# Prompt tokens in three groups (256, 384, 384) instead of four (128, 128, 384, 384), with split operands and the sample tokens in the first

## The chip, the core and the metric

The kernel runs on one core of a Trainium2 chip. The metric is the device time of one execution in microseconds (us); lower is better. Three runs of the kernel before took 4751.45, 4752.73 and 4761.79 us, with a median of 4752.73 us.

## What is computed

One step of a hybrid decoder layer for 1024 prompt tokens and 8 sample tokens of width 1024, in float32. A combined projection feeds three mixers (a state space scan with a convolution of 4 taps, a gated convolution of 31 taps, attention to 256 memory rows); their gated sum is projected and normalised. Then each token picks 128 of 16384 experts and adds what they return. Cut to what matters here:

```python
def _peer_block(t, w_q, sub_keys, u_tab, v_tab):
    qv = (t @ w_q).reshape(nt, PEER_HEADS, 2, PEER_DHALF)
    s = jnp.einsum('thkd,hknd->thkn', qv, sub_keys)
    s_top, i_top = lax.top_k(s, PEER_TOPK)
    ...
    best, pos = lax.top_k(cand.reshape(nt, PEER_HEADS, PEER_TOPK * PEER_TOPK), PEER_TOPK)
    gate = jax.nn.softmax(best.astype(jnp.float32), axis=-1).astype(t.dtype)
    u = jnp.take(u_tab, idx, axis=0)
    act = jax.nn.gelu(jnp.einsum('td,thkd->thk', t, u), approximate=False)
    v = jnp.take(v_tab, idx, axis=0)
    return jnp.einsum('thk,thkd->td', gate * act, v)

def _hybrid_layer(x, ...):
    proj = x @ w_in
    z, xbc, dt_raw, conf_in, q_mem, gates = jnp.split(proj, [...], axis=-1)
    ...
    merged = g[:, :, 0] * branch_a + g[:, :, 1] * branch_b + g[:, :, 2] * branch_c
    x = _layer_norm(ALPHA * x + merged @ w_out, ln1_g, ln1_b)
    x = _layer_norm(ALPHA * x + _peer_ffn(x, ...), ln2_g, ln2_b)
```

The state space scan and both convolutions carry a state from token to token, so the prompt has to be worked through in order.

## The kernel before, in words

**Groups.** The prompt is cut into groups (`GROUPS`), each of which goes through the whole layer up to its experts. `front(g)` (line 442) loads the group's tokens and works out the step sizes; `main(G)` (line 510) runs the mixers and the output projection. Every group loads every weight block anew: 88 blocks of the combined projection (`proj`, line 428), 16 of `wso`, 8 each of `wmo`, `wco` and `wo` (`out_product`, line 487), and 16 of `wq` (`routing`, line 685). A block is 128 x 1024 float32, 512 KB, in one of four buffers (`wr`).

**Products.** `product` (line 189) has two forms. With plain float32 operands (line 197) a block is eight matmuls, each of which the trace shows as two records. With a pair of float32r parts (line 186) the scalar engine rounds the block to `wh` (line 175), the vector engine takes the rest as `wl` (line 177), and three matmuls per eighth, 24 a block, add up `wh xh + wh xl + wl xh`. Before, the projections of groups 0 and 1 (`PLAIN`) are plain, those of the groups of 384 are split; the output products are plain in every group.

**Experts.** For all groups but the last the experts are fetched row by row. A *row* is one of a token's 128 choices for 128 tokens at once: the POOL queue gathers 128 x 1024 float32 from the table (line 404), and the vector engine multiplies and sums it (line 413 for `u`, line 423 for `v`). The 640 tokens of the groups ahead of the last have 640 `u` rows and 640 `v` rows; the samples add 16 of each. Five buffers (`uv`) hold rows. The last group's experts are done densely: `dense_group` (line 1126) multiplies by the whole tables, 128 blocks of each.

**What sets the order.** The program is written as a stream, and a scheduler turns it into one fixed list per engine. Work that fills gaps hangs on queues: `tick` (line 212) emits the next steps of `bg` (the memory's keys and values, then the routing of the group before), `TICKS[g]` steps a chunk of the scan; `side` holds the sample tokens' mixers, `PTICK[g]` steps a projection, from the group after the one with which the samples ride (`RIDE`). `spread` (line 237), called at each product, emits as many expert rows as a rate says: `PHASES[g]` by the part of `main`, `PACE` afterwards. Rows of a group exist once its routing is through. What is left when the dense work has been written is emitted at the end:

```python
    dense_group(G)
    while experts:
        due[0] = 8.0
        spread()
    sample_final()
```

**The samples' convolution state.** `sample_mixers` loads and stores it in three pieces each (lines 886 and 895); a piece is 128 x 64 runs of three floats.

## Time and profile before

| | us |
|---|---|
| median of three runs | 4752.73 |
| span of the profiled execution | 4755.2 |
| lowest, highest run | 4751.45, 4761.79 |
| busy in the span: PE, DVE, ACT, POOL | 4060.0, 3651.7, 1809.1, 1800.8 |

The profiled execution is the span from its first to its last instruction; it lies between the runs' lowest and highest time, so nothing of note lies around it. PE is the tensor engine, PEld its weight loads, DVE the vector engine, ACT the scalar engine, POOL the engine whose queue issues the gathers, SP the one whose queue issues all other transfers. Matmuls overlap in the profile: the start of one to the start of the next says what one costs, not its duration.

### The profile page before, as it was taken

Reading aid. Unit: us, or ns where it says so; the run is one execution under the profiler, and the core shown is the slowest. Engines: PE = TensorE matmul, PEld = TensorE weight load, DVE = VectorE, ACT = ScalarE, POOL = GpSimd, SP = SyncE. Lnnn points to the kernel's source line nnn. Section 1 sums busy time; section 2 is a strip of 40 time slices with the busy share of each in tenths; the row PEclk is TensorE's granted clock in tenths of the full one; section 3 lists DMA queues with packets and bytes.
Section 4 is the critical chain, followed back from the end, with each engine's and each line's share of the span. In section 5 each row is a group of like instructions: output and inputs, shape, how many; then the busy total and the mean of one; then the engine's idle time right before and its main releaser. Section 6 shows DMA issues by size and latency. Waiting matters only on the chain. (4 is left out here: it accounts for less than half of the span.)

```text
span 4755.2 us, 61836 instructions
## 1 busy us (share of the span) xinstructions
PE 4060.0 (85%) x20483; PEld 3296.9 (69%) x20483; DVE 3651.7 (77%) x7682; ACT 1809.1 (38%) x4128; POOL 1800.8 (38%) x1595
## 2 busy tenths in 40 slices
PE   9999961589878899899769898889887899789997
PEld 8999860578666776577448686545555688677886
DVE  1363561668898799789988899879886799788998
ACT  3434420136456332154225432221786333323334
POOL 0000030443533334554134644554111455555663
PEclk9999885889978999989888799889898999999999
DMA  6676689887847877987566876987567999999998
GB/s 200 211 237 223 204 275 52 306 306 258 289 158 233 260 272 268 359 280 251 180 230 209 322 250 221 339 298 266 189 216 268 323 389 389 255 349 366 371 383 300
DMA packets 500161, 1278.29 MB, mean 269 GB/s; under 512 B 111312, under 2 KB 182864, under 8 KB 497664
## 3 DMA queue, kind: packets, MB, share of 16 engines
q0 software_dynamic: 186880, 679.56, 40.7%
q1 hardware_dynamic: 312960, 594.77, 39.3%
q8 instruction: 162, 2.65, 0.2%
q14 instruction: 159, 1.30, 0.1%
HBM read 1220.22 MB, written 53.93 MB: 268 GB/s over the span
## 5 line engine op out<-in xcount | busy, mean ns | idle before, releaser
L404 POOL DMA_INDIRECT uv<-in_peer_u,idx x640 | 789.8, 1234 | 1198.4 <-DVE uv L413 804.5
L404 POOL DMA_INDIRECT uv<-in_peer_v,idx x640 | 841.7, 1315 | 899.6 <-DVE pacc L423 547.8
L413 DVE SCALAR_TENSOR_TENSOR uv<-uv,x 128x1024 f32<-128x1024 f32 (+1 forms) x656 | 789.5, 1218 | 198.9 <-DMA uv<-in_peer_u,idx 186.0
L423 DVE SCALAR_TENSOR_TENSOR pacc<-uv,av,pacc 128x1024 f32<-128x1024 f32 (+1 forms) x650 | 831.9, 1280 | 98.6 <-DMA uv<-in_peer_v,idx 87.4
L186 PE MATMUL mm<-xt,wh 128*128 128x384 f32 x2816 | 790.5, 361 | 22.5 <-ACT b L589 12.7
L197 PE MATMUL mm<-b,wr 128*128 128x128 f32 (+2 forms) x3072 | 746.6, 397 | 32.0 <-ACT b L648 9.9
L197 PEld LDWEIGHTS mm<-b,wr 128*128 128x128 f32 x3072 | 491.8, 200 | 239.5 <-issue 26.1
L175 ACT ACTIVATE wh<-wr 128x1024 fp32r<-128x1024 f32 x274 | 290.2, 1060 | 830.7 <-DMA wr<-in_win 250.1
L186 PEld LDWEIGHTS mm<-xt,wh 128*128 128x128 f32 x2816 | 538.8, 200 | 58.4 <-ACT b L589 17.6
L186 PE MATMUL mm<-xt,wl 128*128 128x384 f32 x1408 | 502.0, 357 | 36.0 <-DVE wl L177 35.9
L197 PE MATMUL mm<-xt,wr 128*128 128x128 f32 (+1 forms) x2816 | 371.7, 292 | 98.2 <-DMA wr<-in_win 91.3
L535 DVE SCALAR_TENSOR_TENSOR b<-raw,cc,b 128x128 f32<-128x128 f32 (+1 forms) x960 | 443.1, 478 | 11.7 <-ACT b L533 4.7
L197 PEld LDWEIGHTS mm<-xt,wr 128*128 128x128 f32 x2816 | 357.7, 204 | 107.7 <-issue 92.3
L177 DVE TENSOR_TENSOR wl<-wr,wh 128x1024 fp32r<-128x1024 f32 x274 | 333.3, 1217 | 32.7 <-ACT wh L175 32.2
L186 PEld LDWEIGHTS mm<-xt,wl 128*128 128x128 f32 x1408 | 280.7, 199 | 47.8 <-DVE wl L177 42.0
L1223 PE MATMUL mm<-wh,b 128*128 128x512 f32 x768 | 246.0, 402 | 16.7 <-ACT b L150 16.4
L150 ACT ACTIVATE b<-acc 128x384 fp32r<-128x384 f32 x128 | 66.7, 525 | 372.7 <-PE st L1223 224.5
L186 PE MATMUL sp<-b,wh 128*128 128x384 f32 x784 | 206.2, 345 | 0.5 <-ACT b L682 0.5
L186 PE MATMUL tp<-b,wh 128*128 128x384 f32 x784 | 202.6, 340 | 0.0
L1162 PEld LDWEIGHTS mm<-e,e 128*128 128x128 f32 x768 | 119.9, 208 | 95.1 <-ACT e L1161 83.8
L1223 PE MATMUL ss<-wh,b 128*128 128x512 f32 x512 | 182.9, 398 | 0.0
L197 PE MATMUL mm<-acc,wr 128*128 128x128 f32 (+3 forms) x640 | 153.0, 402 | 27.0 <-DVE acc L591 12.7
(386 smaller groups left out, 6880.1 us busy)
## 6 DMA issues: line engine op xcount, KB each, us to landing
wr<-in_win SPq DMA_DIRECT2D x352, 512.0 KB, 4.6
wr<-in_peer_ut SPq DMA_DIRECT2D x128, 512.0 KB, 7.1
e<-in_peer_v SPq DMA_DIRECT2D x256, 256.0 KB, 7.2
wr<-in_wso SPq DMA_DIRECT2D x64, 512.0 KB, 4.8
wr<-in_wq SPq DMA_DIRECT2D x64, 512.0 KB, 5.5
gd<-xt SPq DMA_DIRECT2D x16, 1536.0 KB, 5.1
xt<-gd SPq DMA_DIRECT2D x16, 1536.0 KB, 18.9
wr<-in_wmo SPq DMA_DIRECT2D x32, 512.0 KB, 5.2
```

The costliest lines, as they stand in the source:

```text
L150: act.activation(hi, src, AF.Copy)
L175: act.activation(wh, wr, AF.Copy)
L177: dve.tensor_tensor(wl, wr, f32(wh), op=OP.subtract)
L186: pe.matmul(ps, a[:, k], b[k0 + k], start=(i == 0), stop=(i == n - 1))
L197: pe.matmul(ps, w[:, k], xs[k], start=(k == 0), stop=(k == 7))
L404: pool.indirect_dma_start(out=dst, out_offset=None, in_=table, in_offset=bass.IndirectOffsetOnAxis(ap=idx_col, axis=0))
L413: dve.scalar_tensor_tensor(u, u, 1.0, x1, op0=OP.mult, op1=OP.mult, accum_out=av[:, s:s + 1])
L423: dve.scalar_tensor_tensor(acc, v, av[:, s:s + 1], acc, op0=OP.mult, op1=OP.add)
L535: dve.scalar_tensor_tensor(cv, raw[:, i:i + nt], col(C_FW, j * TAPS + i), cv, op0=OP.mult, op1=OP.add)
L1162: pe.matmul(pg[:, u * P:(u + 1) * P], oj[:, u], oi[:, u], start=True, stop=True)
L1223: pe.matmul(outs[2 * tbk + dh], a[:, ts], v[:, dh * 512:dh * 512 + 512], start=(c == 0 and i == 0), stop=(c == P - 1 and i == 2))
```

## The change

The two groups of 128 become one of 256; the groups of 384 stay. No group is plain any more, so the first group's projections are split too. The samples (8 columns) ride with group 0, which makes its projections 264 columns wide; their mixers are emitted in the group after, as before. The rates lose their entry for the second group of 128; those of the groups of 384 and of the dense part are the same. The functions keep their code; line numbers fall by 2 or 3.

```diff
-GROUPS = (128, 128, 384, 384)
+GROUPS = (256, 384, 384)
-PLAIN = (0, 1)
-TICKS = (8, 5, 2, 3)
-PTICK = (0, 0, 1, 0)
+TICKS = (4, 2, 3)
+PTICK = (0, 1, 0)
 PHASES = tuple(dict(zip(("ssd", "out0", "out1", "att", "merge", "rest"), x)) for x in (
     (0, 0, 0, 0, 0, 0),
-    (3.5, 3, 3, 3, 3, 3),
     (2.5, 4.5, 3, 3.5, 3, 2),
     (3.5, 2, 3, 4.5, 1, 3)))
-RIDE = 1
+RIDE = 0
...
-        xt = [xtp.tile([P, 8, N], dt, name="xt") for dt in ((F32,) if g in PLAIN else (F32R, F32R))]
+        xt = [xtp.tile([P, 8, N], F32R, name="xt") for _ in range(2)]
         xt = [[x[:, k, :nx] for k in range(8)] for x in xt]
-        raw = xt[0] if g in PLAIN else [blk(nx) for _ in range(8)]
+        raw = [blk(nx) for _ in range(8)]
         for k in range(8):
             sp.dma_start(raw[k][:, :nt], I["xT"][k * P:(k + 1) * P, G.t0:G.t0 + nt])
             if g == RIDE:
                 act.activation(raw[k][:, nt:], xs_raw[:, k], AF.Copy)
-            if g not in PLAIN:
-                split(raw[k], nx, hl=(xt[0][k], xt[1][k]))
-        G.x = raw if g in PLAIN else tuple(xt)
+            split(raw[k], nx, hl=(xt[0][k], xt[1][k]))
+        G.x = tuple(xt)
```

What the scheduler makes of it at three places. The vector engine's list from the dense part's results (line 1230) to its end, before; `uv` are rows of experts, `wr` the dense results, `x_35560` the samples' result:

```order
L1230 SCALAR_TENSOR_TENSOR wr<-wr,mm 128x512 x3
L390 TENSOR_REDUCE ln2d<-wr 128x1
...
L401 SCALAR_TENSOR_TENSOR wr<-wr,ln2d,wl 128x1024
L398 SCALAR_TENSOR_TENSOR wr<-wr,ln2d,wl 128x1024
L398 SCALAR_TENSOR_TENSOR x_35560<-x_35560,ln2s,uv 8x1024
L401 SCALAR_TENSOR_TENSOR wr<-wr,ln2d,wl 128x1024
L401 SCALAR_TENSOR_TENSOR x_35560<-x_35560,ln2s,uv 8x1024
```

The same stretch of the change (its line 1227 was 1230, its 411 and 421 were 413 and 423):

```order
L1227 SCALAR_TENSOR_TENSOR wr<-wr,st 128x512
L399 SCALAR_TENSOR_TENSOR wr<-wr,ln2d,wl 128x1024
L411 SCALAR_TENSOR_TENSOR uv,av<-uv,x_30912 128x1024
...
L411 SCALAR_TENSOR_TENSOR uv,av<-uv,x_30912 128x1024 x55
L414 TENSOR_TENSOR av<-av,gate_16095 128x128
L419 TENSOR_SCALAR pacc<-uv,av 128x1024
L421 SCALAR_TENSOR_TENSOR pacc<-uv,av,pacc 128x1024
...
L421 SCALAR_TENSOR_TENSOR pacc<-uv,av,pacc 128x1024 x3
...
L421 SCALAR_TENSOR_TENSOR pacc<-uv,av,pacc 128x1024 x123
L1239 SCALAR_TENSOR_TENSOR uv<-uv,pacc 128x1024
```

Before, no row of experts stands behind the dense part's first result; now 62 `u` rows and 128 `v` rows do.

The SP queue around the samples' convolution state (`sconv`), before, at the end of group 1; `wr` are weight blocks:

```order
L169 DMA wr<-in_win 128x1024 x3
L886 DMA sb<-in_sconv 128x64x3
L895 DMA out_sconv<-sb 128x64x3
L169 DMA wr<-in_win 128x1024
L886 DMA sb<-in_sconv 128x64x3 x2
L169 DMA wr<-in_win 128x1024
L895 DMA out_sconv<-sb 128x64x3 x2
L169 DMA wr<-in_win 128x1024
L169 DMA wr<-in_wmo 128x1024
```

And in the change, near the end of group 0:

```order
L167 DMA wr<-in_wco 128x1024
L167 DMA wr<-in_win 128x1024
L883 DMA sb<-in_sconv 128x64x3
L892 DMA out_sconv<-sb 128x64x3
L883 DMA sb<-in_sconv 128x64x3 x2
L892 DMA out_sconv<-sb 128x64x3 x2
L167 DMA wr<-in_wco 128x1024
L167 DMA wr<-in_win 128x1024
```

The same six transfers still stand between weight blocks of the first 256 tokens, now with no block between them.

The vector engine's first rows of experts, before, in group 1, between the chunks of its scan (`acc`, `sp_v` to `sp_w`: output products and the samples' step sizes):

```order
L732 TENSOR_TENSOR sp_v<-sp,dtb 8x32
L413 SCALAR_TENSOR_TENSOR uv,av<-uv,x_5265 128x1024 x4
L577 TENSOR_TENSOR acc<-acc,mm 128x128
L735 TENSOR_SCALAR sp_u<-sp_e 8x32
L413 SCALAR_TENSOR_TENSOR uv,av<-uv,x_5265 128x1024
```

And in the change, in the first group of 384 (`s_xdt`, `s_y`: the samples' state; 128x384: the group's blocks):

```order
L842 TENSOR_TENSOR b<-b 128x384 x4
L175 TENSOR_TENSOR wl<-wr,wh 128x1024 x2
L411 SCALAR_TENSOR_TENSOR uv,av<-uv,x_9274 128x1024
L919 SCALAR_TENSOR_TENSOR sb<-sb,s_xdt 128x128 x2
L922 SCALAR_TENSOR_TENSOR sb,s_y<-sb 128x128
```

The first group of 256 has no rows to run beside; they begin within the group of 384 that follows.

## Rows read from the trace of the kernel before

**Rows 1.** The page's part 2: busy tenths in 40 slices of 119 us.

```profile
PE   9999961589878899899769898889887899789997
```

**Rows 2.** Windows by stage: stretch, its length, busy us (instructions) by engine, clock, DMA.

```profile
0.00:391.40 391.40, 370.86 (x2817) 349.47 (x2818) 147.44 (x486) 133.57 (x363) 14.29 (x71) 0.95 0.68 223
391.40:690.00 298.60, 252.90 (x1842) 232.57 (x1840) 172.00 (x599) 127.04 (x429) 52.54 (x89) 0.88 0.67 237
690.00:857.00 167.00, 44.08 (x261) 40.92 (x261) 36.60 (x118) 16.11 (x48) 18.56 (x21) 0.60 1.28 76
857.00:1012.20 155.20, 103.02 (x713) 97.36 (x712) 109.54 (x268) 23.96 (x72) 71.86 (x64) 0.83 0.96 360
1012.20:1607.00 594.80, 515.42 (x2620) 432.80 (x2621) 496.43 (x1180) 324.35 (x833) 237.84 (x204) 0.87 0.70 239
...
3647.00:4755.20 1108.20, 995.50 (x4684) 860.15 (x4684) 960.59 (x1269) 376.33 (x634) 595.90 (x447) 0.96 0.96 346
```

**Rows 3.** The same windows for tile uv alone; POOL's count is that of gathers issued.

```profile
1012.20:1607.00 594.80, 192.54 (x180) 0.00 (x0) 194.06 (x150) 0.87 0.70 239
...
2043.00:3647.00 1604.00, 584.62 (x689) 2.48 (x4) 582.46 (x461) 0.91 0.71 249
3647.00:4755.20 1108.20, 575.09 (x642) 3.69 (x6) 595.90 (x447) 0.96 0.96 346
```

**Rows 4.** PE's waits from 690 to 857 us: total, times, longest.

```profile
PE mm L197 <- DMA wr<-in_win: 79.4, 2, 78.8
```

**Rows 5.** Transfers from 691 to 857 us.

```profile
DMA packets 52490, 12.47 MB, mean 75 GB/s; under 512 B 49600, under 2 KB 49600, under 8 KB 52485
```

**Rows 6.** Timeline of PE at five places: start, us, line, form, how many in sequence.

```profile
59.65 10.74 PE L197 MATMUL mm<-acc,wr 128*128 128x256 f32 x49
...
78.66 10.88 PE L197 MATMUL mm<-xt,wr 128*128 128x128 f32 x96
...
391.37 11.29 PE L197 MATMUL mm<-xt,wr 128*128 128x136 f32 x96
...
1772.88 0.51 PE L186 MATMUL mm<-xt,wh 128*128 128x384 f32 x2
...
1776.00 0.51 PE L186 MATMUL mm<-xt,wh 128*128 128x384 f32 x2
...
4720.45 0.86 PE L1223 MATMUL mm<-wh,b 128*128 128x512 f32 x3
4721.15 0.39 PE L1223 MATMUL ss<-wh,b 128*128 128x512 f32 x1
```

**Rows 7.** The page's part 5: busy us, mean ns of one, idle before it, what ended that.

```profile
L413 DVE SCALAR_TENSOR_TENSOR uv<-uv,x 128x1024 f32<-128x1024 f32 (+1 forms) x656 | 789.5, 1218 | 198.9 <-DMA uv<-in_peer_u,idx 186.0
L423 DVE SCALAR_TENSOR_TENSOR pacc<-uv,av,pacc 128x1024 f32<-128x1024 f32 (+1 forms) x650 | 831.9, 1280 | 98.6 <-DMA uv<-in_peer_v,idx 87.4
...
L186 PE MATMUL mm<-xt,wl 128*128 128x384 f32 x1408 | 502.0, 357 | 36.0 <-DVE wl L177 35.9
```

**Rows 8.** Timeline of DVE and POOL from 3049.7 us: five rows in sequence and their gathers.

```profile
3049.74 6.56 DVE L423 SCALAR_TENSOR_TENSOR pacc<-uv,av,pacc 128x1024 f32<-128x1024 f32 x5
3051.28 1.86 POOL L404 DMA_INDIRECT uv<-in_peer_v,idx  x1 [2.33 <-DVE pacc L423]
3053.45 1.02 POOL L404 DMA_INDIRECT uv<-in_peer_v,idx  x1 [0.31 <-issue]
3054.77 1.01 POOL L404 DMA_INDIRECT uv<-in_peer_v,idx  x1 [0.30 <-issue]
```

**Rows 9.** The gathers (line 404), all, from issue to landing.

```profile
DMA to landing us min/median/max: 3.8/7.0/39.2
```

**Rows 10.** Groups of POOL from 3000 to 3100 us.

```profile
L404 POOL DMA_INDIRECT uv<-in_peer_v,idx x52 | 60.5, 1163 | 41.4 <-DVE pacc L423 28.6 <-issue 7.3 <-DMA uv<-in_peer_v,idx 2.3
```

**Rows 11.** Timeline of DVE: the last row of experts, and the first dense result.

```profile
4716.31 1.28 DVE L423 SCALAR_TENSOR_TENSOR pacc<-uv,av,pacc 128x1024 f32<-128x1024 f32 x1 [1.12 <-DMA uv<-in_peer_v,idx]
...
4727.95 1.28 DVE L1230 SCALAR_TENSOR_TENSOR wr<-wr,mm 128x512 f32<-128x512 f32 x2
```

## The prediction

> **What bounds the kernel now.** I read the page's slices first, to find where the tensor engine is not full [rows 1]: its first five slices are at 9, the sixth to eighth at 6, 1 and 5. The windows cut that place into stages [rows 2]. Group 0 takes 391.4 us with PE busy for 370.9, so matmuls set its pace. Group 1, which has the same products, runs from 391.4 to 1012.2 us, 621 us for the same work. It carries what group 0 does not: the first rows of experts, and the samples' convolution state. In the stage from 690 to 857 us PE is busy for 44 of 167 us; its longest wait is 78.8 us for a weight block [rows 4], while the queues are full of 49600 packets under 512 bytes [rows 5]. From 1012.2 us on, DVE is the second full engine (496 of 595 us), and at the end all three are near full: PE 996, DVE 961 and the transfers 0.96 of 1108 us [rows 2]. Rows of experts fill what is free from group 1 on, and before they end just ahead of the dense part: the last at 4716.3 us, the first dense result at 4728.0, the end at 4755.2 [rows 11]. So time is won where PE waits in the first 1012 us, and lost where rows no longer fit beside other work.
>
> **The first 256 tokens: removed and added.** Sums are made against the span of 4755.2 us, which is 2.5 us above the median.
>
> *Projections.* A plain record of 128 columns costs 10.88/96 = 0.113 us, one of 136 columns 11.29/96 = 0.118 [rows 6]. 88 blocks of 16 records in each of the two groups: 1408 x 0.113 + 1408 x 0.118 = 325 us. The change has 88 x 24 = 2112 split matmuls of 264 columns. The trace has none of that width. At 384 columns one costs (1776.00 - 1772.88)/18 = 0.173 us, at 512 (4721.15 - 4720.45)/3 = 0.233 [rows 6]. A line through both gives 0.117 at 264; taking off the 384 row 120 columns at 2.4 GHz gives 0.123. I take 0.122, between a floor of 0.113 (the narrow plain record) and a ceiling of 0.173 (no gain from fewer columns). 2112 x 0.122 = 258 us: 67 less.
>
> The Trainium skill, page "TensorE: Matmul & The Clock Gate", section "Back-to-back issue gap", gives columns/2.4 + 2.5 ns, 112.5 ns here. By it the forecast would be 20 us lower. At 384 columns it says 162.5 ns where the row shows 173, so the rows stand.
>
> *Output products.* 40 blocks x 16 records: twice 0.113 before, once 10.74/49 = 0.219 at 256 columns [rows 6]: 640 x (0.226 - 0.219) = 4 us less.
>
> *The stage as a whole.* Group 0 is the clean measure, since no row and no small piece runs in it. Of its 391 us, 56 are the memory's 16 blocks (128 records at 0.219, 256 at 0.113) and some 22 the start before PE is full. What is left, 313 us, is a group's own work with its small waits. Twice 313, plus 56, plus 22, less 71 for the products: 633 us.
>
> *Splitting the blocks.* 88 more roundings and remainders. They lie beside PE: DVE was busy 147 of 391 us in group 0 [rows 2]. What shows is the wait of PE for `wl`, 36 us for 176 blocks [rows 7]. A narrower product covers less of it, so I take 28 us for 88 blocks (0 to 60).
>
> *The convolution state.* The same six transfers stay in the path, now back to back on SP's queue. PE lost 123 us in that stage; with no block between the pieces I take 135 (80 to 160).
>
> Sum: 633 + 28 + 135 = 796 us where 1012 stood: **216 us less**. The other 80 to 90 us are what the rows cost group 1.
>
> **The first group of 384.** Routing is now for 256 tokens instead of 128: 256 query records at 0.219 instead of 0.113 and the keys twice, 30 us of PE, and about 18 us more of DVE for the choice. Rows start only after it: by the change's order 52 rows stand up to the place that before reaches at 1607 us, where 150 were issued in that stage alone [rows 3]. 98 rows fewer at 1.25 us [rows 7] take 122 us from DVE, which is 83% busy there, while PE has 79 us idle. I count half of the 122, less 48: **13 us less** (48 more, if rows were free there, to 74 less, if all of DVE's time counts).
>
> **The middle and the dense part.** The rates are unchanged, and so is what fits. From that place to the first dense result the order has 1070 rows, before some 1054: 461 and 447 in the last two windows [rows 3]. I cost this at nothing; the 16 rows more hide in a DVE that is 87% busy in the dense part [rows 2]; were it full, they would cost 16 x 1.25 = 20 us.
>
> **The tail.** Before, 108 rows ran in group 1 and 150 in the next stage. The change runs 52 of these 258, and nothing later takes up the rest. So 62 `u` rows and 128 `v` rows stand behind the dense part's first result, with nothing beside them. For one row: DVE needs 6.56/5 = 1.31 us, and POOL issues every 1.32 us [rows 8]; that is the floor. The ceiling is 100/52 = 1.92, the fullest 100 us before, where weights shared the queues [rows 10]. Five buffers also set a pace: landing plus 1.28 over five is 1.66 at the median landing of 7.0 us and 1.02 at the fastest of 3.8 [rows 9]. With weights gone I take landing near the middle and 1.45 us, nearer to the floor: 190 x 1.45 = 276 us. The dense results share DVE with them: 8 us. From the last row to the end, normalisation and store take 16 us (4716.3 to 4728.0 and a store). So 300 us follow the first dense result, where 27 did: **273 us more** (249 to 365 for the rows alone).
>
> Sum: -216 - 13 + 273 = +44 us; 4752.7 + 44 = 4797 us.
>
> **Rivals.** *The group of 384 comes free* (faster). Place: the 595 us from 1012.2. If rows and not PE set its pace, PE's part there, 515 us at a mean clock of 0.87, is 448 us at the full clock; with 30 us of queries and the small waits of group 0 (391/371) that is 505 us. The stage then gains 90 us instead of 13, and the sum is 4720, or 4693 with rows at 1.31. It decides once that stage and the front together gain over 273 us. For it: DVE at 83%, clock 0.87. Against it: the samples' state and routing stay there.
>
> *The tail is slower.* Rows at 1.85, as in the fullest stretch before: 76 us more, 4873. For it: landing at 7.0 us and only five buffers. Against it: no other traffic.
>
> *The split brings nothing at this width*, and the change does not do what it says: a 264-column matmul costs 0.173. Then the front loses 2112 x 0.051 = 108 us, 4905. Nothing in the trace says that the cost stops falling below 384 columns, but nothing shows it either.
>
> *POOL and DVE take turns.* A gather that starts while DVE works on a row lasts 1.86 us instead of 1.02 [rows 8]. If each had to wait out a whole row, the pace were 1.28 + 1.02 + 0.3 = 2.6 us and the end 5015. Against it: the following gathers come every 1.32 us while DVE goes on. Such a rule stands in the Trainium skill, "SBUF — State Buffer", section "SBUF: two separate sides": a DVE instruction with two SBUF inputs and a POOL instruction exclude each other. The one long gather agrees; the pace of the rest shows that the turns fit into one row's time.
>
> **How the numbers follow.** Forecast 0.65, group of 384 comes free 0.18, slow tail 0.11, split brings nothing 0.04, turns 0.02. The terms' ends around the forecast (80 to 160 for the stall, 0 to 60 for the splits, 48 more to 74 less for the group of 384, 249 up for the rows) don't all fall on one side; together they give some 60 us to each side, 4737 to 4857. The range goes down to 4700 for the first rival and up to 4885 for the second. A measurement of this kernel tells 0.2%, about 10 us, from no change. Faster by more than that (below 4743) holds the first rival and a little of the forecast: 0.20. Within 10 us: 0.09 out of the forecast. Slower: 0.71.
>
> **What would show it.** In the profile after: split matmuls of 264 columns starting 0.122 us apart; the first product of 384 columns near 800 us; no gather before it; one stall of 100 us or more for a weight block ahead of it; the dense part as long as before; and behind it some 280 us in which PE is idle and rows of 1.4 to 1.5 us follow one another. The prediction is wrong if the front falls below 740 us, if PE is idle for less than 250 us at the end, or if the dense part itself stretches.

## The result, and the profile after

The change makes the kernel slower. Beside each other, four runs of each, the changed kernel took 4882.32 us (4878.27 to 4887.14) and the kernel before 4757.26 us (4751.45 to 4765.36), both medians: ratio 1.0256, 95% interval 1.0239 to 1.0274. The forecast was 4797 us, within 4700 to 4885. So the direction was right, the time is inside the range by 3 us, and the size was wrong: 125 us lost where 44 were forecast. That the time lies inside the range at all is partly luck: a gain in the front 55 us larger than forecast hides part of losses that are 141 us larger (the table below).

The page's part 2 of the changed kernel, its 40 slices of 122 us:

```profile
PE   9999649996889989967899879886898889998100
...
DVE  4457414578779878898789879877698878988777
...
POOL 0000000001424554425454555212365556655776
PEclk9989779997899988988799989898999999999555
DMA  5434993343797997757786888557899999999898
```

Before, PE had its hole in slices 6 to 8 and was full to the end [rows 1]. Now the hole is in slices 5 and 6, and a second one takes the last three slices, where DVE and POOL go on at 7 and the transfers at 8 to 9. POOL's row says when experts are fetched: nothing until slice 10; the first gather starts at 1166 us.

Windows of the changed kernel by stage (stretch, its length, busy us of PE, PEld, DVE, ACT, POOL with their instructions, granted clock, DMA share, GB/s), the answer to [rows 2]:

```profile
0.00:500.00 500.00, 479.33 (x3114) 433.90 (x3115) 269.92 (x524) 261.47 (x638) 23.90 (x69) 0.96 0.45 141
500.00:741.00 241.00, 128.61 (x695) 116.64 (x695) 66.03 (x146) 38.45 (x76) 1.82 (x5) 0.75 1.09 84
741.00:1368.00 627.00, 548.35 (x2721) 458.23 (x2720) 424.50 (x1319) 327.03 (x831) 93.05 (x110) 0.88 0.47 148
...
3416.00:4501.00 1085.00, 979.47 (x4562) 846.15 (x4563) 921.60 (x1238) 355.91 (x596) 603.54 (x440) 0.96 0.97 343
4501.00:4557.00 56.00, 30.25 (x122) 21.97 (x120) 47.90 (x74) 20.76 (x33) 30.32 (x23) 0.81 0.89 317
4557.00:4885.00 328.00, 1.87 (x2) 0.10 (x2) 242.96 (x249) 9.10 (x15) 238.96 (x181) 0.50 0.87 302
```

The last line is the new tail: 328 us in which PE works for 1.9. To add up where the time went I take six marks that both traces have: the instruction that writes the step sizes of the first and of the second group of 384 (line 742, in the change 739), the third convolution block of the first group of 384, the first and the last of the 128 multiplications by the gates in the dense part, and the end.

| stretch | before | after | difference | forecast |
|---|---|---|---|---|
| start to the step sizes of the first group of 384 | 1024.1 | 752.9 | -271 | -216 |
| from there to that group's third convolution block | 582.9 | 615.3 | +32 | -13 |
| the rest of that group | 436.3 | 438.5 | +2 | 0 |
| the last group, its routing and gates | 1603.7 | 1609.1 | +5 | 0 |
| the dense part, first to last weighing | 1053.2 | 1085.7 | +33 | 0 |
| from the last weighing to the end | 54.9 | 383.9 | +329 | +273 |
| span | 4755.2 | 4885.4 | +130 | +44 |

The gain in the front was put too low, and so was every loss behind it. Row steps (one gather, one instruction of DVE) tell the same story: at the last weighing the kernel before had done 1304 of its 1312, the changed one 1107. That is 197 steps more behind it, at 329/197 = 1.67 us each. The forecast counted from other marks: from the first product of 384 columns (1012.2 us before, 746.9 after) and from the first dense result (4728.0 and 4532.7). By these the front gains 265 us for 216, and the tail loses 325 us for 273; behind the first dense result stand 190 row steps, as the order says.

The front's hole: PE's waits (total, times, longest) from 500 to 760 us, ACT's in the same stretch, and the transfers from 544 to 680 us:

```profile
PE mm L184 <- ACT b L586: 103.7, 2, 64.5
```

```profile
ACT wh L173 <- DMA wr<-in_win: 90.5, 8, 71.5
ACT proj_s L895 <- DVE proj_s L894: 44.5, 1, 44.5
```

```profile
DMA packets 41592, 2.56 MB, mean 19 GB/s; under 512 B 41089, under 2 KB 41089, under 8 KB 41591
```

The samples' convolution state still fills all queues for 136 us with short runs that move next to nothing, as in [rows 4, 5]. PE now waits for ACT, which has to round each weight block (line 173; line 586 comes behind that in ACT's list); and ACT, in the order of its list, waits first for the state itself (through the vector engine's convolution of it, 44.5 us) and then for a weight block queued behind it (71.5 us).

The tail, first as groups of POOL and DVE from 4560 to 4880 us (count | busy us, mean ns | idle before, releasers):

```profile
L402 POOL DMA_INDIRECT uv<-in_peer_v,idx x128 | 168.1, 1313 | 47.4 <-issue 28.0 <-DMA uv<-in_peer_v,idx 9.2 <-DVE pacc L421 8.6
L421 DVE SCALAR_TENSOR_TENSOR pacc<-uv,av,pacc 128x1024 f32<-128x1024 f32 x127 | 163.2, 1285 | 51.9 <-DMA uv<-in_peer_v,idx 49.3
```

Then the same rows one by one, from 4779 us (start, us, what, [idle before it <- releaser]):

```profile
4779.12 6.61 DVE L421 SCALAR_TENSOR_TENSOR pacc<-uv,av,pacc 128x1024 f32<-128x1024 f32 x5 [0.57 <-DMA uv<-in_peer_v,idx]
4780.68 1.86 POOL L402 DMA_INDIRECT uv<-in_peer_v,idx  x1 [0.92 <-DVE pacc L421]
4782.84 1.03 POOL L402 DMA_INDIRECT uv<-in_peer_v,idx  x1 [0.30 <-issue]
...
4786.70 1.28 DVE L421 SCALAR_TENSOR_TENSOR pacc<-uv,av,pacc 128x1024 f32<-128x1024 f32 x1 [0.97 <-DMA uv<-in_peer_v,idx]
4786.85 1.96 POOL L402 DMA_INDIRECT uv<-in_peer_v,idx  x1 [0.30 <-DMA uv<-in_peer_v,idx]
4789.00 1.28 DVE L421 SCALAR_TENSOR_TENSOR pacc<-uv,av,pacc 128x1024 f32<-128x1024 f32 x1 [1.01 <-DMA uv<-in_peer_v,idx]
4789.11 1.99 POOL L402 DMA_INDIRECT uv<-in_peer_v,idx  x1 [0.30 <-DMA uv<-in_peer_v,idx]
```

Here the tail's price can be read. A gather takes between 0.94 and 2.00 us, on a mean 1.31, and 0.37 us lie between two (47.4/128); so POOL's gathers and gaps by themselves make 1.68 us. How long one takes depends on DVE: the gather at 4786.85 starts 0.15 us after a row of DVE and ends 0.83 us after that row's end (4787.98); the one at 4782.84 starts just ahead of the end of a row and is through in 1.03. Of the 121 gathers that start between 4655 and 4860 us, 108 start 0.09 to 1.09 us into a row, and each of them ends 0.81 or 0.82 us after the end of that row; the other 13 start between rows or in a row's first 0.08 us and take 0.94 us. DVE in turn idles for the landing of its rows, 49.3 of the 51.9 us.

### The profile page after: what moved, and what is told of

It is laid out like the page before. It is cut to its first block, busy times and chain, and to the rows that moved or that the text cites. A ratio compares the mean times of both kernels' runs of the same rounds, so it can differ in the third digit from the quotient of the medians.

```text
span 4885.4 us, 57373 instructions
## 1 busy us (share of the span) xinstructions
PE 3944.4 (81%) x18755; PEld 3161.2 (65%) x18755; DVE 3706.8 (76%) x7304; ACT 1814.4 (37%) x3932; POOL 1840.1 (38%) x1531
## 4 chain that ended last, share of the span: by engine, by line
issue 17%; DMA 13%; DVE 10%; POOL 8%; PE 8%; ACT 4%; POOLq 0%; DVEq 0%; ACTq 0%
POOL uv L402 8%; DMA uv<-in_peer_v,idx 7%; PE mm L184 3%; DMA uv<-in_peer_u,idx 3%; DVE uv L411 2%; ACT xt L1163 2%; ACT e L1158 2%; DVE pacc L421 2%; PE mm L195 1%; DMA acc<-ad 1%; DVE b L532 1%; DVE wl L175 1%; DVE wl L160 1%; DVE b L314 0%; DVE b L316 0%
## 5 line engine op out<-in xcount | busy, mean ns | idle before, releaser
L184 PE MATMUL mm<-xt,wh 128*128 128x384 f32 (+1 forms) x4224 | 1079.2, 341 | 121.9 <-ACT b L586 113.8
L184 PEld LDWEIGHTS mm<-xt,wh 128*128 128x128 f32 x4224 | 772.7, 199 | 168.1 <-ACT b L586 119.3
L173 ACT ACTIVATE wh<-wr 128x1024 fp32r<-128x1024 f32 x362 | 383.0, 1060 | 1089.4 <-DMA wr<-in_win 377.5
L184 PE MATMUL mm<-xt,wl 128*128 128x384 f32 (+1 forms) x2112 | 711.9, 338 | 41.2 <-DVE wl L175 41.1
L195 PE MATMUL mm<-b,wr 128*128 128x256 f32 (+2 forms) x2304 | 714.3, 464 | 16.0 <-ACT b L645 8.7
L175 DVE TENSOR_TENSOR wl<-wr,wh 128x1024 fp32r<-128x1024 f32 x362 | 441.3, 1220 | 237.2 <-ACT wh L173 234.5
L195 PEld LDWEIGHTS mm<-b,wr 128*128 128x128 f32 x2304 | 443.3, 196 | 233.3 <-issue 16.0
L184 PEld LDWEIGHTS mm<-xt,wl 128*128 128x128 f32 x2112 | 420.8, 199 | 55.4 <-DVE wl L175 47.4
L532 DVE SCALAR_TENSOR_TENSOR b<-raw,cc,b 128x384 f32<-128x384 f32 (+1 forms) x720 | 400.4, 568 | 9.6 <-ACT b L530 4.5
L1220 PE MATMUL mm<-wh,b 128*128 128x512 f32 x768 | 247.2, 403 | 34.0 <-ACT b L148 31.9
L1220 PEld LDWEIGHTS mm<-wh,b 128*128 128x128 f32 x768 | 147.1, 193 | 59.1 <-ACT b L148 32.1
```

The lines of the kernel that those rows point to most:

```text
L173: act.activation(wh, wr, AF.Copy)
L175: dve.tensor_tensor(wl, wr, f32(wh), op=OP.subtract)
L184: pe.matmul(ps, a[:, k], b[k0 + k], start=(i == 0), stop=(i == n - 1))
L195: pe.matmul(ps, w[:, k], xs[k], start=(k == 0), stop=(k == 7))
L532: dve.scalar_tensor_tensor(cv, raw[:, i:i + nt], col(C_FW, j * TAPS + i), cv, op0=OP.mult, op1=OP.add)
L1220: pe.matmul(outs[2 * tbk + dh], a[:, ts], v[:, dh * 512:dh * 512 + 512], start=(c == 0 and i == 0), stop=(c == P - 1 and i == 2))
```

## The experiments

Thirteen kernels ran, in four groups, each with the kernel before on the same chip. The groups differ a little (the kernel before took 4748, 4756, 4759 and 4779 us in them), so whole times are set against before of the same group, and stretches are read from the traces. The theory to start with was that the change trades a front without rows for a tail with nothing but rows, at the tail's price; the rivals were that the dense part holds the loss, and that the stall is the cause.

### Is the loss behind the dense part?

The first run empties the queue of rows in place of the final loop:

```diff
-    while experts:
-        due[0] = 8.0
-        spread()
+    experts.clear()
```

> The changed kernel without the experts' rows that are left after the dense part (190 row steps of the last 128 tokens of the first group of 384, and these tokens' output, are left out). Theory 'tail': all that the change loses lies behind the last dense matmul, where nothing but rows is left; without them the time is what the trace shows up to that matmul (4501.5 us and the 55 us that before needs behind it): 4540 to 4590 us, 290 to 340 below the changed kernel. Rival 'dense part': the rows also hold up the results of the dense part (its last loads and normalisations share DVE with them), and something of the loss stays: 4600 to 4700 us.

It took 4777.0 us (before 4748.0). This misses both, and the fault was in the edit: most of the tail's rows are written out within the dense loop and put behind its work by the scheduler, so only 54 gathers fell away. From the last weighing to the end there were 280.7 us in place of 383.9: 103 less. 54 rows at 1.65 are 89 of these; the other 14 would be that block's normalisation, which falls away with them (15.8 us follow the last row in the changed kernel). The second run cuts by count:

```diff
+        if count[0] >= 1107:
+            experts.clear()
...
+        count[0] += 1
```

> The changed kernel cut off after 1107 of its 1312 row gathers, which are those it had done at the end of the dense matmuls (the last 205 row steps and the output of the 128 tokens they belong to are left out; the run without the final loop had left out 54 only, since the others are written out inside the dense loop and put behind it). Theory 'tail': the loss lies behind the dense part; 4545 to 4590 us. Rival 'dense part': rows that wait in the queue hold the dense part up too, or are held by it; the dense matmuls end at another time than 4501.5 us (more than 15 us off) and the time is 4500 to 4540, or 4600 and more.

It took 4549.1 us (before 4756.5), with the last weighing at 4494.5 us.

```profile
core 0: 4547.3 us, clock 0.913
```

The span (from the list of cores) is 338 us below the changed kernel's. The trace has 1111 gathers, so 201 row steps are left out and not 205: 1.68 us each with the block's normalisation in it. From the last weighing to the end there are 52.8 us, before 54.9; the dense part kept its length, 1084 us. So rows that wait behind the dense part don't stretch it, and the loss is the tail's but for the 30 us or so by which the dense part is longer than before in this run too.

### What sets the pace in the tail?

Three runs touch only the 54 row steps of the final loop. The first lets every second row use a weight buffer, so nine take turns; the second lets ACT scale the `v` rows; the third does both.

```diff
+        if tail and s % 2:
+            return wp.tile([P, D], F32, name="wr", bufs=WRB)
...
+            u = row(s)[:pn]
...
+            v = row(s)[:pn]
...
+    tail.append(1)
```

> The changed kernel with every second row of the tail gathered into the four weight buffers that are idle there, so that nine row buffers take turns in place of five. Theory 'buffers': a row waits until DVE gives one of five buffers back; with nine the rows pace falls from 1.65 us to GpSimd's own gather and gap, 1.3 to 1.4 us, and the time by 45 to 65 us (4820 to 4840). Theory 'GpSimd beside DVE': GpSimd's gather instruction itself takes 1.3 us beside a busy DVE, against 1.0 us elsewhere, and its gap of 0.30 us comes on top; buffers change nothing: 4875 to 4890 us, pace 1.62 to 1.67 us.

```diff
-            if s == 0:
+            if tail:
+                act.activation(v, v, AF.Copy, scale=av[:, s:s + 1])
+            elif s == 0:
...
+    tail.append(1)
```

> The changed kernel with the v rows of the tail scaled by ACT in place of DVE's multiply and add (the sums over these v rows, 128 of the 190 steps, are left out). Theory 'GpSimd beside DVE': with DVE idle GpSimd's gather goes back to 0.94 to 1.05 us, the pace of the v rows to 1.25 to 1.35 us, and the time falls by 40 to 50 us (4832 to 4845). Theory 'transfers': the DMA queues set the pace (one row of 512 KB in 1.65 us), the gather instruction is only waited for; gather and pace stay as they are, and the time within 10 us of the changed kernel. Theory 'buffers': gather stays at 1.3 us, the pace falls by what ACT is faster than DVE, 0.2 us or less.

> The changed kernel with both edits at the 54 row steps of its final loop: nine buffers in turn, and ACT scaling the v rows in place of DVE's multiply and add (their sums are left out). Alone, the one brought these rows from 1.68 to 1.52 us, the other to 1.53. Theory 'two limits, one above the other': with both away GpSimd's 0.94 us and its gap of 0.30 are left, or the transfers at the 371 GB/s that the dense part reaches, 1.41 us for 512 KB: pace 1.25 to 1.43 us, the time 4 to 15 us below the run with ACT alone. Rival 'transfers at 1.52': both edits ran into the same limit, the queues' rate for gathered rows with nothing beside them; pace 1.50 to 1.54 us, no gain over either.

They took 4869.8 and 4855.3 us (before 4748.0), and 4871.8 us (before 4778.6): 1.0256, 1.0226 and 1.0195 of before. 54 rows are little in the whole time, so the pace is read from POOL's groups over some 48 of these rows; busy and idle time by the count is the pace. The changed kernel from 4777 to 4857 us:

```profile
L402 POOL DMA_INDIRECT uv<-in_peer_v,idx x48 | 63.1, 1315 | 17.6 <-issue 10.7 <-DMA uv<-in_peer_v,idx 3.9 <-DVE pacc L421 3.0
```

Nine buffers, 4764 to 4836 us:

```profile
L402 POOL DMA_INDIRECT wr<-in_peer_v,idx x23 | 30.4, 1321 | 9.5 <-issue 6.4 <-DVE pacc L428 3.1
L402 POOL DMA_INDIRECT uv<-in_peer_v,idx x25 | 25.5, 1020 | 7.6 <-issue 7.6
```

ACT in place of DVE, 4755 to 4828 us:

```profile
L402 POOL DMA_INDIRECT uv<-in_peer_v,idx x49 | 46.0, 938 | 28.6 <-ACT uv L421 26.5 <-issue 2.1
```

Both, 4784 to 4843 us, and a window of it (the columns as above):

```profile
L402 POOL DMA_INDIRECT wr<-in_peer_v,idx x24 | 23.3, 970 | 7.3 <-issue 5.2 <-ACT wr L426 1.2 <-DMA wr<-in_peer_v,idx 0.9
L402 POOL DMA_INDIRECT uv<-in_peer_v,idx x23 | 21.6, 941 | 7.0 <-issue 5.8 <-DMA wr<-in_peer_v,idx 0.9 <-DMA uv<-in_peer_v,idx 0.3
```

```profile
4800.00:4820.00 20.00, 0.00 (x0) 0.00 (x0) 0.00 (x0) 17.97 (x16) 15.12 (x17) 0.50 1.03 409
```

The paces are 80.7/48 = 1.68, 73.0/48 = 1.52, 74.6/49 = 1.52 and 59.2/47 = 1.26 us. The first two runs each miss. With nine buffers the pace falls, but by half of what "buffers" wanted, and not because POOL waits less for a buffer (with five it hardly does, 3.0 of 80.7 us): its gathers get shorter, on the mean 55.9/48 = 1.16 us in place of 1.31. With ACT the gather goes back to 0.94 us as "GpSimd beside DVE" said, but then POOL waits 26.5 us for ACT to give buffers back, and the pace stops at 1.52. Only with both gone does it fall to 1.26, which is the gather and its gap; 512 KB at the 409 GB/s of that window are 1.28 us, so these runs don't tell POOL and the queues apart there. Neither limit is the tail's alone: DVE beside the gathers costs 0.16 us a row with five buffers and 0.26 with nine, and four more buffers are worth 0.16 beside DVE and 0.26 beside ACT. The forecast's 1.45 was not to be had by one of the edits alone.

### What does a row cost in the front?

The kernel before without rows in its second group of 128:

```diff
-    (3.5, 3, 3, 3, 3, 3),
+    (0, 0, 0, 0, 0, 0),
```

> The kernel before with no experts' rows in its second group of 128 tokens (all six rates of that group at 0); its some 105 rows must then find a place later. Theory 'rows are cheap in the front' (what they cost there is hidden by the wait for the sample tokens' state): the first 384-group's step sizes come less than 15 us earlier, and the rows are added to the end at 1.65 us each: 4757 + 173 = 4915 to 4935 us. Theory 'rows are dear in the front': they hold DVE there, the step sizes come 40 to 80 us earlier, and the end is 4850 to 4895 us.

It took 4856.5 us (before 4748.0): "dear in the front", and by more than the 40 to 80 us expected. Its windows, from the step sizes of that group to those of the first 384:

```profile
349.70:690.00 340.30, 308.91 (x2407) 289.56 (x2406) 172.28 (x640) 144.07 (x485) 21.95 (x65) 0.92 0.65 216
690.00:907.90 217.90, 99.70 (x767) 97.04 (x766) 58.38 (x187) 28.08 (x77) 8.29 (x13) 0.69 1.18 130
```

The first 384-group's step sizes come at 907.9 in place of 1024.1 us. So 99 row steps (105 against 6 by that mark) cost 116 us there, 1.17 each, and the last weighing leaves 125 steps behind it in place of 8, which takes the end from 54.9 to 250.6 us: 1.67 each. This one run does by itself most of what the change does at the end, and 116 of the change's 271 us in the front. The stall stays (DMA at 1.18 in the second line). The dense part is longer here too, 1107 us in place of 1053, with the same groups as before: it stretches when rows move back, and doesn't need the merged group for it.

### Is it the stall that separates the two?

The samples' state in whole runs, in both kernels:

```diff
-            sp.dma_start(win[:, :, :, 0:3], I["sconv"][:, js])
+            cx = sb()
+            ci, co = cx[:, 0:192], cx[:, 192:384]
+            sp.dma_start(ci, I["sconv"][:, js].rearrange("p j b t -> p (j b t)"))
+            pool.tensor_copy(win[:, :, :, 0:3], ci.rearrange("p (j b t) -> p j b t", j=8, b=8))
...
-            sp.dma_start(O["sconv"][:, js], win[:, :, :, 1:4])
+            pool.tensor_copy(co.rearrange("p (j b t) -> p j b t", j=8, b=8), win[:, :, :, 1:4])
+            sp.dma_start(O["sconv"][:, js].rearrange("p j b t -> p (j b t)"), co)
```

> The kernel before with the samples' convolution state (24 x 8 x 3 values a partition) loaded and stored in whole runs of 768 B, and spread to and from the windows of four by copies on GpSimd, in place of runs of 12 B. Theory 'short runs': the 12 B runs hold all queues between 691 and 857 us of before, where PE is busy a third of the time; without them 100 to 140 us go there, and as the later parts are full of work the end moves by 90 to 140: 4620 to 4665 us. Rival 'hidden': the rows that were gathered under the stall then share the time with other work, and 40 us or less are left: 4715 to 4760 us.

> The same edit in the changed kernel. Theory 'the stall is in both and as long': it comes between 545 and 680 us, no rows run beside it, PE is busy 129 of 241 us from 500 to 741; 100 to 130 us go and the end moves by as much: 4750 to 4785 us, and the changed kernel stays 90 to 140 us behind before with the same edit. Rival 'the stall is what separates the two': the changed kernel gains over 40 us more from the edit than before does.

Before with it: 4647.8 us, 0.9789 of before (0.9749 to 0.9829). The changed kernel with it: 4765.3 us, 1.0024 (1.0008 to 1.0039). The first is the window from 690 to 857 us of before with whole runs, to be set beside the third line of [rows 2]; the second the changed kernel's from 500 to 741 us:

```profile
690.00:857.00 167.00, 110.97 (x781) 103.67 (x780) 124.77 (x341) 33.87 (x105) 82.24 (x78) 0.84 0.88 325
```

```profile
500.00:741.00 241.00, 234.60 (x1318) 209.10 (x1318) 118.66 (x300) 112.99 (x261) 7.07 (x23) 0.96 0.40 128
```

In the changed kernel the hole is gone; in before PE is busy for 111 of these 167 us in place of 44. The step sizes of the first 384 come 118 us sooner before (906.5) and 117 sooner after (635.5). The two kernels stay 117 us apart, where they were 125. So the stall is no part of the difference, within some 10 us, and it is worth 2% to either.

### What is the split worth?

The changed kernel with its first group in plain float32 (its operands not split, one weight form):

```diff
+PLAIN = (0,)
...
-        xt = [xtp.tile([P, 8, N], F32R, name="xt") for _ in range(2)]
+        xt = [xtp.tile([P, 8, N], dt, name="xt") for dt in ((F32,) if g in PLAIN else (F32R, F32R))]
...
+            if g not in PLAIN:
...
```

> The changed kernel with its first group of 256 multiplied as plain float32 (no split). The forecast put 256 plain columns at some 0.430 us a matmul and three split ones of 264 at 0.366, 8 each for 88 projections and 48 blocks behind: 40 to 75 us more in the front, and, since all rows come after it, as much at the end: 4920 to 4960 us. Rival 'split brings nothing' (its splitting on ACT and DVE and the weight loads hold PE as long as it saves): 4875 to 4895 us. Rival 'clock': longer matmuls, no idle: the same 40 to 75 us at another place.

It took 4915.7 us (before 4756.5), a little under the expected band. Its timeline on PE, one plain block of 264 columns and its neighbours:

```profile
363.78 3.72 PE L196 MATMUL mm<-xt,wr 128*128 128x264 f32 x16
367.34 3.62 PE L196 MATMUL mm<-b,wr 128*128 128x256 f32 x16
```

A plain block takes 3.56 us from start to start; a split one of 24 matmuls, 0.120 us apart in the median of the changed kernel's trace, 2.88. 88 blocks at 0.68 are 60 us. Of these 27.5 reach the first 384-group's step sizes (780.4 against 752.9 us) and 28.5 the end of the span. The rest, some 32 us, would be what the splitting costs, for which the forecast had 28 and which the expectation had left out. It is a difference of single traces: in the seven with this front unchanged the mark lies between 738.1 and 757.3 us, so the rest is 18 to 37 us.

### Can the rows start sooner?

The changed kernel with its background steps in the first group of 384 at eight a chunk, so that the routing is written out sooner:

```diff
-TICKS = (4, 2, 3)
+TICKS = (4, 8, 3)
```

> The changed kernel with its background steps in the first group of 384 at eight a chunk in place of two, so that the 16 queries and the routing of the 256 tokens are written out in the group's first three chunks; nothing else. In the changed kernel the first row is gathered at some 1190 us, 440 us after that group began, with the DMA at 0.34 to 0.42 until then. Theory 'late routing': the tail is long since no row can start before; the rows start 150 to 250 us sooner, 90 to 150 of the 205 row steps leave the tail at 1.65 us, and cost 0 to 1.1 us each where they go: the end is at 4700 to 4820 us. Rival 'rates': rows are held by the rates of the phases and the share of DVE; a sooner start moves the same rows and gives back what it gains: 4850 to 4890 us.

It took 4808.6 us (before 4759.2): 1.0104, "late routing". The windows of tile uv alone (busy us of DVE, ACT and POOL; POOL's count is that of gathers), from the step sizes of the first 384 to its third convolution block, of the changed kernel and of this run:

```profile
753.00:1368.00 615.00, 62.54 (x104) 0.00 (x0) 73.79 (x57) 0.88 0.48 149
```

```profile
743.00:1404.00 661.00, 147.67 (x244) 0.00 (x0) 161.26 (x127) 0.86 0.59 196
```

70 gathers more lengthen this stretch by 46 us, 0.66 each; 85 steps fewer stand behind the last weighing (120 in place of 205), which takes 241 us in place of 384. The last group and the dense part are 15 and 17 us longer in this run; whether the rows do that wasn't tried, but with it the 85 steps cost some 0.9 us each. Both kernels have one place where DVE works through the choice of the best keys in one piece and PE stands, for 50 us of each (the changed kernel, then this run):

```profile
1150.00:1200.00 50.00, 12.61 (x56) 11.55 (x57) 49.05 (x153) 8.63 (x16) 9.31 (x9) 0.55 0.33 101
```

```profile
900.00:950.00 50.00, 9.23 (x38) 7.62 (x39) 50.00 (x164) 5.36 (x9) 7.91 (x6) 0.55 0.24 81
```

The kernel before has a place of this kind for its 128 tokens, where PE stands for 18 of 25 us:

```profile
1410.00:1435.00 25.00, 6.92 (x30) 5.34 (x29) 24.05 (x72) 6.95 (x16) 0.00 (x0) 0.61 0.09 26
```

### The best of each

Three versions put these together. Before, with the convolution branch's state in whole runs too (a load and a store of 960 B a partition with a copy on POOL, as above):

> The kernel before with both sample states (the state space's in 12 B runs, and the convolution branch's in 120 B runs) moved in whole runs. The run with the first alone came to 4648 us. Theory 'every short run holds the queue': the 16 transfers of 1024 runs of 120 B take 50 us of all queues; as they lie where PE is busy and the DMA at 0.7, 10 to 40 us more go: 4605 to 4640 us. Rival 'hidden': they have room, nothing more goes: 4640 to 4660 us.

The changed kernel with both states in whole runs, `TICKS = (4, 8, 3)`, and the routing written out per 128 tokens:

```diff
-            route(P, tb, 8, sv, si, G.idx, G.gate)
-            experts.extend(peer_block(g, c, G.idx, G.gate) for c in range(tb))
+            for c in range(tb):
+                route(P, 1, 8, *([x[:, c:c + 1] for x in t] for t in G.top), G.idx[:, c:c + 1], G.gate[:, c:c + 1])
+                experts.append(peer_block(g, c, G.idx, G.gate))
+                yield
```

> The changed kernel with both states in whole runs, routing per 128 tokens, and eight background steps a chunk in its first group of 384. If the stall (120 us) and the late routing (80 to 150 us) add up: 4600 to 4690 us, level with before with whole runs (4648 us). If the rows that start sooner take from DVE what PE needs, as 1.1 us a row in the second group of before: 4690 to 4760 us.

And that with higher rates of rows:

```diff
-TICKS = (4, 8, 3)
+TICKS = (4, 8, 6)
...
-    (2.5, 4.5, 3, 3.5, 3, 2),
-    (3.5, 2, 3, 4.5, 1, 3)))
+    (3, 4.5, 3.5, 3.5, 3.5, 3),
+    (3.5, 3, 3, 4.5, 2, 3)))
```

> The changed kernel with whole runs, routing per 128 tokens and early routing (4679 us, 108 row steps behind the last weighing), and higher rates of rows in the phases where they were low (first group of 384: 3, 4.5, 3.5, 3.5, 3.5, 3; last: 3.5, 3, 3, 4.5, 2, 3; background steps 6 a chunk in the last). Theory 'rates': 60 to 108 row steps leave the tail at 1.65 us and cost 0.66 us where they go (what 70 rows cost the first group of 384 in the run with early routing): 4575 to 4630 us, level with before with whole runs or better. Rival 'no room': DVE is busy for 86 to 90% there, a row costs the 1.25 us that DVE works on it or more, and the time stays within 25 us: 4655 to 4705 us.

| kernel | us | ratio to before (95%) |
|---|---|---|
| before, both states in whole runs | 4630.8 | 0.9727 (0.9709 to 0.9745) |
| changed, whole runs and early routing | 4678.8 | 0.9826 (0.9806 to 0.9846) |
| the same with higher rates | 4649.4 (before 4778.6) | 0.9742 (0.9700 to 0.9783) |

The first beats both kernels. The second did what the sum of its parts asked for; the routing in pieces didn't remove the place where PE stands for DVE (38.7 us of PE's waits for `wl` from 637 to 1000 us), so its own share isn't shown. The third fits neither theory. The rates moved no rows: 105 steps stand behind its last weighing, 108 without them. Yet it is some 0.8% faster, and the traces put that in the dense part (1073 us in place of 1108). DVE waits 71 us for `u` rows in that part, in place of 99; why wasn't tried and stays open. With it the merged group is level with four groups, by ratios whose intervals overlap.

## Why the prediction was right and wrong

**The sign and the mechanism held.** The front shrank, one stall stayed in it, no gather came before the routing, rows piled up behind the dense part, and that cost more than the front gave. None of the rivals came true as it was told; the slow tail came nearest, with 1.85 us a row (its "fullest stretch before" is 1.92 by the prediction's own ceiling). And one of the signs by which the prediction called itself wrong came: the dense part stretched.

**The tail: the step that failed, by its price.** The prediction put the tail between a floor of 1.32 us and a ceiling of 1.92 and wrote "With weights gone I take landing near the middle and 1.45 us, nearer to the floor". The number of rows was right: 190 stand behind the first dense result. They took 327.9 us, from 4541.7 to 4869.5, of which some 6 are normalisations of the dense results: 1.69 us a row in place of 1.45, 46 us more than the 276. The rest of the term held but for 7 us: 9 + 6 us for the dense results where 8 were taken, and 15.8 us behind the last row where 16 were. The prediction's row for five buffers at the median landing said 1.66 [rows 9]; that it comes so near is chance, since five buffers without DVE beside the gathers give 1.52. What sets the price is both together, gathers that DVE lengthens and five buffers. Two reasons were there to be seen. The floor came from five rows in sequence [rows 8], in which the gathers happen to start just ahead of the end of a row; the first gather of that same group, 1.86 us long, was taken as an exception, where in the tail all lengths from 0.94 to 2.00 us occur and their mean is 1.31. And the nearest rows were not used: 190 steps at the end of the program, with only rows beside them, are unlike a streak in the middle, but the mean of 52 gathers there, 1163 ns and 41.4/52 of idle time [rows 10], already said that POOL is not at 1.02.

The rival of turns was weighed with the Trainium skill, page "SBUF — State Buffer", section "SBUF: two separate sides": whichever of the two starts first keeps the shared ports for its whole instruction. For the gathers the trace agrees, by the 108 that end 0.81 or 0.82 us after the row they started in, and by 0.94 us for a gather beside ACT; that DVE in its turn is held by a gather, the trace doesn't show. What the prediction made of it, 2.6 us a row as turns added up, was too much, and what it concluded against it, that "the turns fit into one row's time", was too little: the rows of DVE are not lengthened (1.285 us on the mean), only the gathers are, by 0.37 us on the mean.

**The front: -271 for -216.** The steps "the stage as a whole" and "splitting the blocks" gave 661 us for a front without the stall, up to the first product of 384 columns; with whole runs that product comes at 629.5, 31 less. The stall is 117 where 135 were taken. The 264-column matmul is 0.120 us where 0.122 was taken. So the sum was 49 us too cautious, and the other 6 are the way from that product to the step sizes, 12 us before and 6 after. Which part of the 31 us was too high isn't shown. What rows cost enters this sum nowhere, since it starts from a measured 1012 us; the remark beside it, that rows cost group 1 "80 to 90 us", has no working, and the run without rows gives 116.

**The first group of 384: +32 for -13.** Half of DVE's 122 us, 61, was counted for 98 rows that go, and 48 against it for the larger routing, 30 of PE and 18 for the choice. PE's own work grew by 31 us there (536.4 in place of 505.4 us, read in windows between the marks), as forecast, and that is the +32: PE's idle time stayed, 78.7 us in place of 77.6, though the rows had gone. The longest of its waits there (total, times, longest), before and after, are those for the choice of the best keys:

```profile
PE sp L910 <- ACT sb L913: 20.7, 4, 18.1
```

```profile
PE sp L907 <- ACT sb L910: 34.6, 2, 32.8
PE tp L837 <- DVE e L823: 14.9, 1, 14.9
```

The two waits of 32.8 and 14.9 us end at 1188.5 and 1154.6 us, while DVE works through the choice for 256 tokens in one piece; before, the choice for 128 cost one of 18.1. So the choice took 30 us more, where 18 were counted, and all other waits together fell by 28: that is the most that the 97 rows gave back at PE, where 61 were counted. By the 0.66 us a row of the run with early routing they would have given 64; why it was less isn't shown.

**The dense part: +33 for 0.** The same number of rows runs in it (442 steps, before 444), so more rows are not the reason. PE idles 18 us more between the two marks (105 in place of 87), and is busy 14 us longer with the same products, at a mean granted clock of 0.962 of 2.4 GHz in place of 0.970. PE's waits in it, by releaser, before and after:

```profile
PE mm L1223 <- DVE wl L162: 29.6, 12, 9.4
PE sp L186 <- DVE wl L177: 25.5, 19, 4.6
PE tp L186 <- DVE wl L177: 18.6, 14, 3.1
PE mm L1223 <- ACT b L150: 16.4, 1, 16.4
```

```profile
PE sp L184 <- DVE wl L175: 32.9, 17, 4.4
PE mm L1220 <- ACT b L148: 31.9, 1, 31.9
PE tp L184 <- DVE wl L175: 30.0, 19, 4.4
PE mm L1220 <- DVE wl L160: 27.6, 17, 5.5
```

The waits for ACT, 16.4 and 31.9 us, end a microsecond behind the first weighing and belong to the stretch ahead of it. The others, all for DVE's `wl`, sum to 74 and 90 us: 17 of the 33. In the same stretch DVE's wait for `u` rows to land went from 41.6 to 68.5 us, and DVE, which takes its work in order, then has `wl` late for PE. The other traces bear this out:

| traces | DVE's wait for `u` rows in the dense part, us | its length, us |
|---|---|---|
| before, and its two versions with whole runs | 42 to 51 | 1053 to 1064 |
| the changed kernel, and its seven versions with the same rows there | 69 to 75 | 1081 to 1090 |
| the last version, with higher rates | 71 | 1073 |
| before without rows in its second group; early routing, alone and with whole runs | 87 to 99 | 1102 to 1108 |

The two go together. What makes the rows land later no run tried, and it is not the number of `u` rows alone: the last version has 272 of them in the dense part, as many as the three below it.

By the six marks the terms add up: 55 us more gained in the front, and 56, 45, 33 and 7 us more lost behind it, make 130 of +44.

## What to carry to other kernels

Work that fills gaps has a price in each place: here a row cost 0.66 us in the first group of 384, 1.17 in the second group of 128, and some 1.7 alone at the end; a change that empties a front of fillers has to be charged with the difference. A floor read from a fortunate streak is no forecast: take the mean of the longest stretch that is bound by the same thing, and where two limits (buffers, the issuing engine) lie close, expect the price of both together: 1.68 us here, where either alone left 1.52. And look for transfers of very short runs: here runs of 12 B held all 16 queues for 136 us to move 2.56 MB, and moving them whole and spreading them on an engine with room was worth 2%, where the change under study cost 2.6%.

## What was not expected of the hardware

- Short runs: 41592 packets with 2.56 MB took 136 us of all 16 queues; that is 136 x 16/41592 = 52 ns a packet on each. In whole runs the stall of 117 us vanished.
- A gather that starts 0.09 to 1.09 us into a row of DVE (1.285 us, two inputs) ends 0.81 us after that row's end, in 108 of 108 cases in the tail; beside ACT it takes 0.94 us. DVE's own instruction is not lengthened.
- With nine buffers and ACT, rows of 128 x 4 KB were gathered at 1.26 us, 409 GB/s, above the 380 GB/s that the changed kernel's dense part shows at most in a slice, beside weights and stores.
- A plain block of 264 columns takes 3.56 us where three times as many split matmuls take 2.88, so the split still pays at that width: 60 us on PE for 88 blocks, some half of which (18 to 37 us) didn't reach the end of the front.
